# Thirteen up-projection chunks by seven products, ten of them from raw kept sums, and token sums formed in the residual's own rows

## The chip, the cores and the metric

One core of a Trainium2 chip runs the whole block. Its engines work side by side from their own queues: TensorE (PE, with weight loads PEld), VectorE (DVE), ScalarE (ACT), GpSimd (POOL) and SyncE (SP, which here only issues DMAs). The metric is the device time of one execution in microseconds, the median of several.

## The reference, cut to what matters

One layer of an encoder block over 512 frames of width 1024, all in float32. The change lies in the last line but one, and in what prepares it.

```python
def conv_glu(x, w_up, conv_w, conv_b, w_down):
    hid = x @ w_up                                  # (512 x 1024) @ (1024 x 5632)
    hid = causal_depthwise_conv3(hid, conv_w) + conv_b
    gate, up = hid[..., :2816], hid[..., 2816:]
    return (silu(gate) * up) @ w_down

def reference(x, ...):
    proj = rms_norm(x, norm1_g) @ w_in
    out_a = chunked_attention(...)                  # 8 heads
    out_b = stick_breaking_attention(...)           # 8 heads
    mixed = sigmoid(gate_a) * (out_a @ w_branch_a) + sigmoid(gate_b) * (out_b @ w_branch_b)
    x = x + mixed @ w_out
    x = x + conv_glu(rms_norm(x, norm2_g), w_ffn_up, ffn_conv_w, ffn_conv_b, w_ffn_down)
    return x
```

## The kernel before

Every float32 matrix is split into a rounded half (`hi`, by an ACT cast) and a remainder (`lo`, by a DVE subtraction), and a product is three PE products: hi by hi, hi by lo, lo by hi. Weights come in chunks of 1 MB through `load` (SP), are split by `split_gen` one chunk ahead, while the chunk before is multiplied, and are used by a body; `run_chunk` advances the split by one piece at each `yield` of the body. The order of instructions on each engine is fixed when the kernel is built, by a scheduler that goes by priority and its own estimate of times.

**Stages.** Input projection and both attentions (to about 300 us), the branch and output projections (`yB`, `wo`, to 378), the second norm with transposes (`norm_T`), the up-projection (22 chunks `up0` to `up21`, 378 to 606), the down-projection (606 to the end).

**The up-projection.** Chunk `up{j}` holds 128 columns of the gate and the same 128 of the up half. A plain chunk (`up_body`) computes both over 512 tokens: 2 x 8 blocks x 3 products of 512 columns. A chunk in `SEVEN` (`up_seven`) treats the pair as a 2 x 2 block matrix (halves of the contraction by gate and up) and the tokens as two halves of 256, and computes it with seven block products instead of eight: 7 x 4 x 3 products of 256 columns. It needs sums of weight blocks and sums of token blocks.

**Sums of weights, "parking".** In the attention stage `park_gen` loads each chunk of `SEVEN`, forms four sums on DVE and stores them in the DRAM tensor `parked`. Most chunks pass through one buffer, `pkr`; later odd ones through `pks`. `park()` takes one step at a time, at low priority, 44 times in attention, then twice at each yield of `yB` and `wo`. For a chunk in `SUMS` three of the sums are stored raw (6 steps); for the others they are stored already split (8 steps). In the up stage `fetch_extra` brings them back into a pair of buffers (`w2h`, `w2l` for chunks in `SECOND`, else `wxh`, `wxl`), one chunk ahead of the split if the buffers' last user is at least three chunks back, otherwise at the split's start; `split_seven` then splits raw ones, with two more casts and two more subtractions.

**Sums of tokens.** `norm_T` transposes the normalised rows, `xn`, into `ps`, splits them into `hth` and `htl`, and copies `ps` once more, into `xf`, which POOL stores in the DRAM tensor `htd`. `token_sums` loads it again as `xT` (SP), forms four sums (DVE) and splits them into the four `ts` tiles. `late["ts"]` is this generator, advanced at points of `up0` to `up3`. The residual rows `x2` are stored in DRAM (`x2d`, SP) and read again near the end; their place (`xs` in the pool `cp`) is given up when the pools of the attention stage close, and the pool `fp` is laid over them.

**After a chunk.** `conv` takes three taps (one on ACT, two on DVE); the gate goes to `cg`, of which there is one, and through SiLU; `up_fin` multiplies into `ub`. For each pair of chunks `pair_sums` prepares the down-projection's inputs `ax`, `ay`: `sums` on DVE at once (they use the one tile `st`), and the split, `by_dma`, as a debt in `owed` that `pay()` settles later: eight ACT copies and four POOL DMAs that add in place. In a seven-product chunk ACT saves three partial products in `pc`; `behind` keeps other ACT work that is named there (weight casts, a debt's copies) after these copies.

Of the kernel before, what the change touches and what calls it, by code (L numbers as in the profile page):

```python
# [8 lines left out]
F32 = mybir.dt.float32  # L9
# [58 lines left out]

SEVEN = (4, 5, 7, 8, 10, 11, 13, 14, 16, 17, 18, 20)
SUMS = (11, 13, 14, 16, 17, 18, 20)  # L70
SECOND = (5, 8, 11, 14, 17)


@with_exitstack
def block_kernel(ctx: ExitStack, tc: tile.TileContext, x, xt, params, g2, rbx, wts, wd0, wd1, out):
# [9 lines left out]
    hp = h_ctx.enter_context(tc.tile_pool(name="hp", bufs=1, side="right"))  # L85
    cp = ap_ctx.enter_context(tc.tile_pool(name="cp", bufs=1))

# [230 lines left out]
    dram = ctx.enter_context(tc.tile_pool(name="dram", bufs=1, space=bass.MemoryType.DRAM))  # L318
    htd = dram.tile([NT, 2, P, S], F32, tag="htd", name="htd")
    ayd = dram.tile([7, P, 1536], F32, tag="ayd", name="ayd")  # L320
# [41 lines left out]
    def norm_T(src, xn, gain, t, psum, nm):  # L362

        ss = pool_c.tile([P, 1], F32, tag="ss", name=f"ss_{nm}{t}", bufs=2)
        dump = pool_st.tile([P, D], F32, tag="skh", name=f"dump_{nm}{t}", bufs=2)
        A.activation(dump, src, AF.Square, accum_out=ss)
        rs = rstd_of(ss, 1, D, f"rs_{nm}{t}")
        for b in range(2):
            cs = slice(b * 512, (b + 1) * 512)
            V.scalar_tensor_tensor(xn[:, cs], src[:, cs], rs[:, 0:1], gain[b], op0=ALU.mult, op1=ALU.mult)  # L370
            ps = psum(f"tp_{nm}{t}{b}")
            for k in range(4):
                PE.transpose(ps[:, k * P:(k + 1) * P], xn[:, (4 * b + k) * P:(4 * b + k + 1) * P], ident)
            p3 = ps.rearrange("p (k q) -> p k q", k=4)
            hv = hth[:, 4 * b:4 * b + 4, t * P:(t + 1) * P]
            A.copy(hv, p3)
            V.tensor_tensor(htl[:, 4 * b:4 * b + 4, t * P:(t + 1) * P], p3, hv.bitcast(F32), op=ALU.subtract)

            xf = pool_wk.tile([P, S], F32, tag="wa", name=f"xf_{nm}{t}{b}", bufs=5)
            A.copy(xf, ps)  # L380
            G.dma_start(htd[t, b], xf)

# [634 lines left out]
    def pair_sums(i):  # L1017
# [5 lines left out]
        if i < 8:  # L1023
            ax = fp.tile([P, 2048], F32R, tag="ax", name=f"ax{i}", bufs=6)
            ay = fp.tile([P, 1536], F32R, tag="ay", name=f"ay{i}", bufs=2)
# [47 lines left out]
    def keep_place(i):  # L1073
# [6 lines left out]
        if ("t", j) not in keep:  # L1080
            keep["t", j] = fp.tile([P, 2048], F32, tag=("w2l", "ax")[j], name=f"t2_{j}", bufs=(1, 6)[j])
        return keep["t", j][:, (i - 3) % 4 * 512:(i - 3) % 4 * 512 + 512]

    def up_fin(j, pg, pu, g=None):
# [5 lines left out]
        if j % 2 == 1 and j // 2 < 9:  # L1090
# [8 lines left out]
            owed.append(rest_)  # L1099
            if j == 17:  # L1100
                owed.pop()()

# [8 lines left out]
    def up_body(j):  # L1111
        def body(hi, lo):
            pg, pu = BANK(f"pg{j}", j - 1), BANK(f"pu{j}", j - 1)
            yield from up_mm(pg, hi, lo, 0, 0, S)
            g = gate(j, pg)
            if j in (2, 3):
                next(late["ts"])
            held = [] if j + 1 in SEVEN else None
# [8 lines left out]
            else:  # L1127
                end()
            if j % 2 == 0:
                pay()  # L1130
            if j in (2, 3):
                next(late["ts"])
        return body

    def fetch(i):

        tag = {0: "wxh", 1: "wxl", 6: "ax"}.get(i, "ts")
        n, bufs = {"wxh": (1600, 1), "wxl": (1600, 1), "ts": (2048, 4), "ax": (2048, 6)}[tag]
        ay = fp.tile([P, n], F32R, tag=tag, name=f"ay{i}", bufs=bufs)[:, 0:1536]
# [7 lines left out]
    def token_sums():  # L1147

        x = []
        for i in range(2):  # L1150
            x.append(fp.tile([P, 2, 1024], F32, tag="ax", name=f"xT{i}", bufs=6))
            for t in range(2):
                for b in range(2):
                    SP.dma_start(x[i][:, b].rearrange("p (k q) -> p k q", k=4)[:, :, t * P:(t + 1) * P],
                                 htd[2 * i + t, b].rearrange("p (k q) -> p k q", k=4))
        b11, b21, b12, b22 = x[0][:, 0], x[0][:, 1], x[1][:, 0], x[1][:, 1]
        yield
        V.tensor_tensor(b22, b22, b12, op=ALU.subtract)
# [7 lines left out]
        for i, src in ((1, b12), (3, b22), (2, b11), (4, b21)):  # L1166
            t = fp.tile([P, 2, 1024], F32R, tag="ts", name=f"ts{i}", bufs=4)
            A.copy(t[:, 0], src)
            V.tensor_tensor(t[:, 1], src, t[:, 0].bitcast(F32), op=ALU.subtract)
            ts[i] = [t[:, j].rearrange("p (k q) -> p k q", k=4) for j in range(2)]  # L1170
            yield

    def up_seven(j):
        def body(hi, lo, wh, wl):
# [31 lines left out]
            yield  # L1206
            if j % 2 == (j - j % 2 in SEVEN and j - j % 2 + 1 in SEVEN):
                late["copied"] = (third,)
                pay()
# [20 lines left out]
    def up_first(j):  # L1230
        def body(hi, lo):
# [4 lines left out]
            if j == 1:  # L1236
                n = 0
                for i, (h, l, g, u) in enumerate(halves):
                    for o, ps in ((0, g), (P, u)):
                        for _ in up_mm(ps, h, l, o, 256, S):  # L1240
                            n += 1
                            if n == 1 or 4 <= n < 8:
                                next(late["ts"])
                            yield
# [57 lines left out]
    def fin0(p):  # L1302
# [3 lines left out]
        if p != 5:  # L1306
            tmp["k"] = fp.tile([P, 4, S], F32, tag="ax", name=f"k{p}", bufs=6)
        tmp[p] = tmp["k"][:, 2:4, :] if p == 5 else tmp["k"][:, 0:2, :]
# [72 lines left out]
    def steps1():  # L1381
        tmp["x"] = [fp.tile([P, 2, D], F32, tag="ax", name=f"x_{r}", bufs=6) for r in range(2)]
        for t in range(NT):
# [74 lines left out]
```

## Time and profile before

| | us |
|---|---|
| median of three runs (714.78 to 715.87) | 715.56 |
| the profiled execution | 717.0 |
| its span, first to last instruction | 715.3 |
| PE busy / DVE / ACT / POOL in the span | 708.5 / 588.7 / 431.7 / 85.9 |
| up-projection, from the first product of `up0` to the first of the down-projection | 378.0 to 605.8 |

The granted clock of TensorE was 0.999 of full speed. Busy times are unions of intervals; PE's are modelled and overlap, so that 99% doesn't say that no gap is left: gaps are read from what the weight loads waited for, and from the starts of consecutive products. A row of instructions reads: line, engine, operation, output <- inputs by tile name, sizes, count, then the busy time in us and the mean in ns, then the idle time of the engine ahead of them and who ended it. A row of a timeline reads: start, length, engine, line, operation, tiles, count, and the idle time ahead of it in brackets. A row by stretch gives, for each of PE, PEld, DVE, ACT and POOL, the busy time and the count, then the clock, the DMA engines' share and GB/s. In the list of waits the numbers are the total in us, how many, and the longest.

### The profile page before, as it was taken

The numbers are of one execution on the slowest core, as the hardware profiler recorded it, in microseconds if no ns is written. First come the engines' busy times: TensorE is split into PE (matmuls) and PEld (weight loads), VectorE is DVE, ScalarE is ACT, GpSimd is POOL, SyncE is SP. The second block draws the span as 40 slices with busy tenths as digits, with TensorE's granted clock in tenths as the row PEclk, the third lists the DMA queues.
The fourth block names the chain that finished last, engine by engine and source line by source line (L and its number), as shares of the span: only waits on it lengthen the run. The fifth ranks groups of instructions, "written<-read, shape, count | busy, mean of one in ns | idle before, by whom it ended". The sixth has DMA issues, their size and how long they took to land.

```text
span 715.3 us, 11278 instructions
## 1 busy us (share of the span) xinstructions
PE 708.5 (99%) x4091; PEld 622.1 (87%) x4091; DVE 588.7 (82%) x1049; ACT 431.7 (60%) x803; POOL 85.9 (12%) x123
## 2 busy tenths in 40 slices
PE   9999999999999999999999999999999999999997
PEld 7889998888988888888889989899899988888885
DVE  6668878796999999769566599698898878998686
ACT  6576656667876776434236457777877765544531
POOL 2501200000121211000003001220311111000000
PEclk9999999999999999999999999999999999999999
DMA  8722235444434383685957857998987799564563
GB/s 318 267 97 89 80 127 187 181 163 159 177 122 161 131 296 119 220 308 185 359 223 294 278 194 271 328 328 263 284 260 195 214 277 398 200 235 173 178 208 118
DMA packets 51864, 154.98 MB, mean 217 GB/s; under 512 B 5600, under 2 KB 12384, under 8 KB 44000
## 3 DMA queue, kind: packets, MB, share of 16 engines
q1 hardware_dynamic: 44256, 133.67, 52.7%
q0 software_dynamic: 7264, 20.45, 10.8%
q8 instruction: 32, 0.52, 0.3%
q14 instruction: 24, 0.20, 0.1%
q10 hardware_dynamic: 288, 0.14, 0.1%
HBM read 116.49 MB, written 30.41 MB: 205 GB/s over the span
## 4 chain that ended last, share of the span: by engine, by line
PE 87%; DVE 5%; DMA 2%; ACT 2%; issue 1%; SPq 1%; POOL 0%; DVEq 0%; ACTq 0%
PE P L1291 15%; PE p L1185 12%; PE vA L440 3%; PE uA L440 3%; PE gB L307 2%; PE qkB L309 2%; PE gB L308 2%; PE gB L309 2%; PE qkB L307 2%; PE qkB L308 2%; PE wo L308 2%; PE wo L309 2%; PE wo L307 2%; PE gA L307 2%; PE gA L308 2%; PE gA L309 2%
## 5 line engine op out<-in xcount | busy, mean ns | idle before, releaser
L172 ACT CAST whi_dn<-raw_dn 128x1024 fp32r<-128x1024 f32 x33 | 34.3, 1051 | 24.8 <-PE P L1291 20.4
L168 DVE TENSOR_TENSOR wlo_dn<-raw_dn,whi_dn 128x1024 fp32r<-128x1024 f32 x33 | 40.0, 1223 | 5.8 <-ACT whi_dn L172 5.8
L1291 PE MATMUL P<-whi_dn,ax 128*128 128x512 f32 x144 | 44.5, 389 | 0.0
L1291 PE MATMUL P<-whi_dn,ay 128*128 128x512 f32 x132 | 40.8, 389 | 0.0
L744 POOL TENSOR_SCALAR_AFFINE_SELECT bB<-bB 128x128 f32<-128x128 f32 x32 | 21.8, 686 | 143.6 <-DVE bB L743 135.0
L214 DVE TENSOR_TENSOR pkr<-pkr 128x512 f32<-128x512 f32 x40 | 27.5, 687 | 9.0 <-issue 4.7
L1185 PE MATMUL p<-ts,whi_up 128*128 128x256 f32 x192 | 34.1, 277 | 0.2 <-ACT pc L1203 0.2
L308 PE MATMUL pg<-htl,whi_up 128*128 128x512 f32 (+1 forms) x96 | 34.0, 354 | 0.0
L309 PE MATMUL pg<-hth,wlo_up 128*128 128x512 f32 (+1 forms) x96 | 33.9, 353 | 0.0
L307 PE MATMUL pg<-hth,whi_up 128*128 128x512 f32 (+1 forms) x96 | 33.8, 353 | 0.0
L1291 PEld LDWEIGHTS P<-whi_dn,ax 128*128 128x128 f32 x144 | 27.0, 188 | 5.6
L308 PE MATMUL pu<-htl,whi_up 128*128 128x512 f32 (+1 forms) x90 | 31.5, 350 | 0.0
L307 PE MATMUL pu<-hth,whi_up 128*128 128x512 f32 (+1 forms) x90 | 31.5, 350 | 0.0
L309 PE MATMUL pu<-hth,wlo_up 128*128 128x512 f32 (+1 forms) x90 | 31.4, 349 | 0.0
L1185 PEld LDWEIGHTS p<-ts,whi_up 128*128 128x128 f32 x192 | 29.2, 188 | 0.7 <-ACT pc L1203 0.4
L1291 PEld LDWEIGHTS P<-whi_dn,ay 128*128 128x128 f32 x132 | 24.8, 188 | 5.1
L250 DVE TENSOR_TENSOR wlo_up<-raw_up,whi_up 128x1024 fp32r<-128x1024 f32 x24 | 29.0, 1221 | 0.3 <-ACT whi_up L249 0.3
L742 DVE TENSOR_TENSOR_SCAN aB<-aB,reset 128x127 f32<-128x127 f32 (+3 forms) x32 | 25.9, 818 | 2.6 <-ACT aB L737 2.5
L1291 PE MATMUL P<-wlo_dn,ax 128*128 128x512 f32 x72 | 28.0, 389 | 0.0
L1185 PE MATMUL p<-hth,whi_up 128*128 128x256 f32 x96 | 26.8, 279 | 0.7 <-ACT pc L1195 0.7
L283 DVE TENSOR_TENSOR wlo_up<-raw_up,whi_up 128x1024 fp32r<-128x1024 f32 (+1 forms) x26 | 24.6, 974 | 2.8 <-ACT whi_up L278 2.7
L1185 PE MATMUL p<-hth,wlo_up 128*128 128x256 f32 x96 | 26.5, 276 | 0.0
(350 smaller groups left out, 2542.3 us busy)
## 6 DMA issues: line engine op xcount, KB each, us to landing
parked<-pkr SPq DMA_DIRECT2D x45, 256.0 KB, 2.5
raw_dn<-in_wd SPq DMA_DIRECT2D x11, 1024.0 KB, 4.8
pkr<-in_wts SPq DMA_DIRECT2D x10, 1024.0 KB, 6.9
raw_up<-in_wts SPq DMA_DIRECT2D x10, 1024.0 KB, 7.5
raw_up<-in_wts SPq DMA_DIRECT2D x12, 512.0 KB, 6.2
raw_dn<-in_wd SPq DMA_DIRECT2D x11, 512.0 KB, 3.6
wxl_up<-parked SPq DMA_DIRECT2D x21, 256.0 KB, 6.0
ayd<-ay POOLq DMA_DIRECT2D x7, 768.0 KB, 5.9
```

Of the source, the lines that this page charges most:

```text
L168: chain("halves", V.tensor_tensor(o, x, y, op=op))
L172: chain("casts", A.copy(hi[:, sl], src))
L214: V.tensor_tensor(b[o], b[x], b[y], op=op)
L250: V.tensor_tensor(l[:, sl], src[:, sl], h[:, sl].bitcast(F32), op=ALU.subtract)
L283: V.tensor_tensor(lo[:, sl], raw[:, sl], hi[:, sl].bitcast(F32), op=ALU.subtract)
L307: ins = PE.matmul(ps, sh, mh, start=first, stop=False)
L308: PE.matmul(ps, sh, ml, start=False, stop=False)
L309: PE.matmul(ps, sl, mh, start=False, stop=last)
L440: PE.matmul(pss[t], st[:, 4 * half + k, t * P:(t + 1) * P], mv[:, k, :], start=half == 0 and k == 0 and j == 0, stop=half == 1 and k == 3 ...
L742: V.tensor_tensor_scan(ar, ar, reset[:, S - n:S - 1][:, ::-1], 1.0, op0=ALU.mult, op1=ALU.max)
L1185: mm = PE.matmul(ps, st, mv[:, k, :], start=first and k == 0 and n == 0, stop=last and k == 3 and n == 2, skip_group_check=True)
L1291: chain("products", PE.matmul(dst, st, mv, start=first and n == 0, stop=last and n == 2, skip_group_check=True))
```

## The change

Chunk 12 joins `SEVEN`. Chunks 8, 10 and 12 join `SUMS`: their sums are kept raw. `SECOND`, which chunk uses which pair of buffers, is dealt anew. `htd`, its stores and its loads go: `norm_T` copies the transposed block into the residual's own rows (`src`, which is `x2`), and `token_sums` takes its blocks from there, with all its steps in the second half of `up1`. The pool `cp` stays open; its place `xs` later holds `ax4` and `ax5` together and then the residual that is read again, and the ring `ax` has four places instead of six. The conditions under which `pay()` is called are new.

```diff
-SEVEN = (4, 5, 7, 8, 10, 11, 13, 14, 16, 17, 18, 20)
-SUMS = (11, 13, 14, 16, 17, 18, 20)
-SECOND = (5, 8, 11, 14, 17)
+SEVEN = (4, 5, 7, 8, 10, 11, 12, 13, 14, 16, 17, 18, 20)
+SUMS = (8, 10, 11, 12, 13, 14, 16, 17, 18, 20)
+SECOND = (5, 8, 11, 13, 16, 18)
...
-    cp = ap_ctx.enter_context(tc.tile_pool(name="cp", bufs=1))
+    cp = ctx.enter_context(tc.tile_pool(name="cp", bufs=1))
...
-    htd = dram.tile([NT, 2, P, S], F32, tag="htd", name="htd")
...
-            xf = pool_wk.tile([P, S], F32, tag="wa", name=f"xf_{nm}{t}{b}", bufs=5)
-            A.copy(xf, ps)
-            G.dma_start(htd[t, b], xf)
+            A.copy(src[:, cs], ps)
...
-            ax = fp.tile([P, 2048], F32R, tag="ax", name=f"ax{i}", bufs=6)
+            if i == 4:
+                keep["ax"] = cp.tile([P, 4096], F32R, tag="xs", name="ax45")
+            if i in (4, 5):
+                ax = keep["ax"][:, 2048 * (i - 4):2048 * (i - 3)]
+            else:
+                ax = fp.tile([P, 2048], F32R, tag="ax", name=f"ax{i}", bufs=4)
...
             owed.append(rest_)
-            if j == 17:
-                owed.pop()()
...
-            if j in (2, 3):
-                next(late["ts"])
...
-            if j % 2 == 0:
+            if j % 2 == 0 and j + 1 not in SEVEN or j == 19:
                 pay()
-            if j in (2, 3):
-                next(late["ts"])
...
     def token_sums():
-        x = []
-        for i in range(2):
-            x.append(fp.tile([P, 2, 1024], F32, tag="ax", name=f"xT{i}", bufs=6))
-            for t in range(2):
-                for b in range(2):
-                    SP.dma_start(x[i][:, b].rearrange("p (k q) -> p k q", k=4)[:, :, t * P:(t + 1) * P],
-                                 htd[2 * i + t, b].rearrange("p (k q) -> p k q", k=4))
-        b11, b21, b12, b22 = x[0][:, 0], x[0][:, 1], x[1][:, 0], x[1][:, 1]
-        yield
+        b11, b21, b12, b22 = [x2[:, 2 * i:2 * i + 2, 512 * b:512 * b + 512] for i in range(2) for b in range(2)]
...
         for i, src in ((1, b12), (3, b22), (2, b11), (4, b21)):
             t = fp.tile([P, 2, 1024], F32R, tag="ts", name=f"ts{i}", bufs=4)
-            A.copy(t[:, 0], src)
-            V.tensor_tensor(t[:, 1], src, t[:, 0].bitcast(F32), op=ALU.subtract)
+            hi, lo = (t[:, j].rearrange("p (k t q) -> p t k q", k=4, t=2) for j in range(2))
+            src = src.rearrange("p t (k q) -> p t k q", k=4)
+            A.copy(hi, src)
+            V.tensor_tensor(lo, src, hi.bitcast(F32), op=ALU.subtract)
...
-            if j % 2 == (j - j % 2 in SEVEN and j - j % 2 + 1 in SEVEN):
+            if (j % 2 or j + 1 not in SEVEN) and j < 18:
                 late["copied"] = (third,)
                 pay()
...
-                            if n == 1 or 4 <= n < 8:
-                                next(late["ts"])
+                            next(late["ts"])
                             yield
...
-        tmp["x"] = [fp.tile([P, 2, D], F32, tag="ax", name=f"x_{r}", bufs=6) for r in range(2)]
+        x = cp.tile([P, 2, 2, D], F32, tag="xs", name="x_")
+        tmp["x"] = [x[:, r] for r in range(2)]
```

The other tiles of the ring `ax` (`t2_1`, `ay6`, the `k` tiles) get four places in the same way. By the new conditions debts are paid in chunks 2, 5, 7, 8, 11, 13, 14, 17 and 19; before, in 2, 5, 6, 8, 11, 12, 14, 17 and at the end of 17.

More of the change, by code (lines that the diff above doesn't have):

```diff
@@ L1080, in keep_place @@
         if ("t", j) not in keep:
-            keep["t", j] = fp.tile([P, 2048], F32, tag=("w2l", "ax")[j], name=f"t2_{j}", bufs=(1, 6)[j])
+            keep["t", j] = fp.tile([P, 2048], F32, tag=("w2l", "ax")[j], name=f"t2_{j}", bufs=(1, 4)[j])
         return keep["t", j][:, (i - 3) % 4 * 512:(i - 3) % 4 * 512 + 512]
@@ L1137, in fetch @@
         tag = {0: "wxh", 1: "wxl", 6: "ax"}.get(i, "ts")
-        n, bufs = {"wxh": (1600, 1), "wxl": (1600, 1), "ts": (2048, 4), "ax": (2048, 6)}[tag]
+        n, bufs = {"wxh": (1600, 1), "wxl": (1600, 1), "ts": (2048, 4), "ax": (2048, 4)}[tag]
         ay = fp.tile([P, n], F32R, tag=tag, name=f"ay{i}", bufs=bufs)[:, 0:1536]
@@ L1306, in fin0 @@
         if p != 5:
-            tmp["k"] = fp.tile([P, 4, S], F32, tag="ax", name=f"k{p}", bufs=6)
+            tmp["k"] = fp.tile([P, 4, S], F32, tag="ax", name=f"k{p}", bufs=4)
         tmp[p] = tmp["k"][:, 2:4, :] if p == 5 else tmp["k"][:, 0:2, :]
```

## The prediction

> **What bounds the kernel now.** I read the page's head, then the chain by engine, then tables by stretch, then the waits of TensorE.
>
> ```profile
> span 715.3 us, 11278 instructions
> PE 708.5 (99%) x4091; PEld 622.1 (87%) x4091; DVE 588.7 (82%) x1049; ACT 431.7 (60%) x803; POOL 85.9 (12%) x123
> PE 87%; DVE 5%; DMA 2%; ACT 2%; issue 1%; SPq 1%; POOL 0%; DVEq 0%; ACTq 0%
> 550.00:570.00 20.00, 20.00 (x178) 20.00 (x178) 17.99 (x30) 16.04 (x30) 3.45 (x4) 1.00 0.65 205
> 610.00:650.00 40.00, 40.00 (x178) 33.13 (x177) 38.33 (x51) 18.49 (x22) 1.06 (x2) 1.00 0.60 202
> 547.79 0.28 PE L1185 MATMUL p<-ts,wxl_up 128*128 128x256 f32 x1
> 548.81 0.28 PE L1185 MATMUL p<-ts,wlo_up 128*128 128x256 f32 x1
> ```
>
> TensorE (PE) is busy throughout and the chain runs through it for 87%, so time is won in two ways only: fewer products, or fewer gaps between them. Products follow each other at a pace; their printed 0.28 us overlaps. From 547.79 to 548.81 nine 256-column products start: 0.1133 us each. The two stretches hold the same 178 products, of 256 columns in 20 us and of 512 columns in 40 us, at clock 1.00, so a 512-column product takes 0.2267.
>
> Where does PE wait in the up-projection? These are the waits of the weight loads from 423 to 606 us; the lines are the copies `pc` by which ScalarE (ACT) saves a partial product.
>
> ```profile
> PEld p L1185 <- ACT pc L1195: 1.1, 2, 0.7
> PEld p L1185 <- ACT pc L1203: 0.4, 1, 0.4
> PEld p L1185 <- ACT pc L1199: 0.3, 1, 0.3
> ```
>
> That is 1.8 us: 1.1 in chunk 4 (0.4, 0.3, 0.4) and 0.7 in chunk 7. I call chunk j what the program calls `up{j}`.
>
> **Part 1: chunk 12 by seven products.** A plain chunk is 2 x 8 x 3 = 48 products of 512 columns: 10.88 us. A seven-product chunk is 7 x 4 x 3 = 84 of 256: 9.52 us. The difference, 1.36 us, comes off the bound engine: -1.36, and no row gives a way to lose it on PE itself. The Trainium skill speaks against it: TensorE: Matmul & The Clock Gate, section Back-to-back issue gap, gives a sustained spacing of 81 ns at 128 columns and 131 ns at 512, so halving the columns doesn't halve the time. Between them my estimate for 256 is 98 ns: 84 x 98 = 8.2 against 48 x 131 = 6.3 us, a loss of 1.9 us. The two stretches above show exact halving here, so I give that rule no chance.
>
> **Part 2: raw kept sums for 8, 10 and 12.** In the attention stage (parking) 8 and 10 lose three casts and three subtractions each, 12 gains four sums. VectorE (DVE) has 4 - 6 = -2 instructions there, ACT -6, SP's queue six 256 KB stores fewer but a 1024 KB load and four stores more. Attention's PE waits for none of it: 0, but for the end of parking (part 5). In exchange chunks 7, 9 and 11 get the casts and subtractions of the next chunk's sums, and 12 its five sums.
>
> ```profile
> L250 DVE TENSOR_TENSOR w2l_up<-w2l_up,w2h_up 128x1024 fp32r<-128x1024 f32 x3 | 3.6, 1216 | 0.0
> L250 DVE TENSOR_TENSOR w2l_up<-w2l_up,w2h_up 128x512 fp32r<-128x512 f32 x3 | 2.1, 686 | 0.0
> L1211 DVE TENSOR_TENSOR hu<-p,pc 128x256 f32<-128x256 f32 x12 | 5.0, 420 | 0.1
> L992 DVE SCALAR_TENSOR_TENSOR cg<-hg,par,cg 128x511 f32<-128x511 f32 x12 | 9.0, 748 | 2.5 <-ACT cg L990 2.4
> L249 ACT CAST wxh_up<-wxl_up 128x512 fp32r<-128x512 f32 x4 | 2.5, 620 | 0.0
> L249 ACT CAST wxh_up<-wxl_up 128x1024 fp32r<-128x1024 f32 x4 | 4.2, 1053 | 0.0
> L1203 ACT COPY pc<-p 128x256 f32<-128x256 f32 x12 | 4.5, 374 | 0.0
> 454.60:605.80 151.20, 150.66 (x1083) 140.86 (x1082) 129.84 (x204) 108.41 (x186) 30.09 (x39) 1.00 0.92 285
> 545.40:574.70 29.30, 29.30 (x257) 29.17 (x256) 26.03 (x42) 21.91 (x40) 4.01 (x5) 1.00 0.69 204
> ```
>
> DVE: 3 x (1.22 + 0.69) + 5 x 0.42 = 7.8 us; ACT: 3 x (1.05 + 0.62) + 4 x 0.37 = 6.5. From 454.6 to 605.8 DVE goes from 129.8 of 151.2 (86%) to 137.6 of 149.3 (92%), ACT from 72 to 77%. The cover is DVE's idle time, and it is uneven: 10 to 14 become five such chunks in a row, where before there were at most three (16 to 18). In chunks 10 to 13 DVE has three casts' remainders of 1.22 and one of 0.69, five sums, four taps of 0.75, a product of 0.69 and half a pair's four sums: 11.0 us by durations, some 9.7 by pace (sixteen instructions that overlap by 0.08, as the four of 0.68 do that take 2.48 in part 5), against 9.52 of PE. Four such chunks lose 0.7 us. If DVE also idles as in 16 to 18 (29.30 - 26.03 = 3.3 in three chunks, 1.1 each) it ends 5.1 us behind, less about 2 that it has spare in the plain chunk 9. Bounds: 0 to 3.1. I take +0.4, near the lower end: in the last stretch quoted PE is busy 29.30 of 29.30, under the same load, and a bank of PSUM is wanted again only two chunks later.
>
> Late fetches: 12, 13, 14 and 18 take buffers used two chunks earlier, so their sums are loaded only in the chunk before; now 18 and 20 do.
>
> ```profile
> 554.22 0.80 SPq L237 DMA_DIRECT2D wxl_up<-parked  x2
> 559.22 1.06 ACT L249 CAST wxh_up<-wxl_up 128x1024 fp32r<-128x1024 f32 x1
> ```
>
> For 18 the load is issued at 554.2 and cast at 559.2 without a wait; the chunk starts near 564.5. Slack 5 us less a cast and a subtraction: 0.
>
> **Part 3: token sums in place.** The eight stores to `htd` (POOL) and eight loads `xT` (SP) go; the eight ACT copies stay, with another target; the sums' twelve instructions keep their sizes, in runs of 128 elements or more.
>
> ```profile
> 394.24 6.43 SPq L1154 DMA_DIRECT2D xT<-htd  x8
> 406.54 1.23 DVE L1158 TENSOR_TENSOR xT<-xT 128x1024 f32<-128x1024 f32 x1 [4.87 <-DMA xT<-htd]
> 390.40:406.50 16.10, 16.10 (x124) 15.29 (x123) 5.52 (x9) 7.42 (x11) 1.09 (x2) 1.00 0.78 232
> 427.83 0.77 ACT L990 ACTIVATE ub<-pu,par 128x512 f32<-128x512 f32 x1
> 428.51 0.62 ACT L1014 ACTIVATE cg<-cg 128x512 f32<-128x512 f32 x1
> 429.03 0.36 ACT L1195 COPY pc<-p 128x256 f32<-128x256 f32 x1
> 386.93 1.27 ACT L380 COPY xf_n<-tp_n 128x512 f32<-128x512 f32 x2
> 377.90 1.76 SPq L941 DMA_DIRECT2D x2d<-x  x2
> DMA to landing us min/median/max: 2.7/4.6/5.9
> ```
>
> Before, the first sum starts at 406.54, held 4.87 us by the reload that SP issues from 394.24 on. Now the rows are ready when the last copy ends, near 391. In 390.4 to 406.5 DVE is busy 5.52 of 16.10, so 10.6 us stand free, and the sums' eight DVE instructions of 1.23 need 9.8. DVE's queue after 406.5, which held up the taps and SiLU that stand ahead of the first `pc` copy on ACT (429.03, behind the SiLU of 428.51), shrinks by about that. So chunk 4's 1.1 us should go: -1.1, bounds 0 (ACT is blocked by something else) and -1.1. What is late next is chunk 7.
>
> The change adds a wait: the copy into the residual's rows must wait until the store of these rows (`x2d`, the last line: its landings) has read them. The last two are issued from 377.90 on and the second by 379.7; at most 5.9 later, 385.6, they have landed; the copies come at 386.93. Slack 1.3 us, and behind the copy on ACT stands the next cast of the transposed input, for which PE waits. Bounds 0 to 2 (a landing as late as that again by half), taken as 0. With the stores, POOL loses eight issues and SP eight; what SP issues next (the first kept sums, read from chunk 4 on) comes earlier, and nobody waits for it: 0. The residual's 16 KB are kept and later hold `ax4`, `ax5` and the reloaded residual, while the ring `ax` has four places for six; `ax6` and `ax7` follow `ax0` and `ax1`, which go to DRAM as before: 0.
>
> **Part 4: the order of the debts (`pay`).** Pair 2's split (eight ACT copies, four accumulating DMAs) moves from chunk 6 into chunk 7, behind the third `pc`.
>
> ```profile
> 447.19 9.50 DMA ay<-st
> 456.82 0.44 DVE st L1044
> 461.19 0.52 ACT cg L1014
> 461.70 0.27 ACT pc L1195
> ```
>
> This is the chain up to the 0.7 us gap: an accumulating DMA of 9.50 us frees `st`, DVE forms the pair's sums, ACT's copies of the debt follow, then a SiLU, then `pc` at 461.70, and PE. The debt leaves that queue; the wait for `st` and the SiLU behind DVE stay. Bounds 0 and -0.7; I take -0.5, since eight ACT copies stood between `st` and `pc` and one SiLU remains. The other debts move between seven-product chunks of like load; chunks 11 and 13 will carry a debt and a full split, which chunk 17 carries now inside the stretch without gaps: 0. Pair 8's debt moves from the end of 17 to 19, where ACT ran it anyway.
>
> **Part 5: the end of parking.** All parked chunks but the last odd ones pass one buffer, `pkr`, and DVE serves it in its order.
>
> ```profile
> 338.37 0.33 SPq L209 DMA_DIRECT2D pkr<-in_wts  x1
> 355.35 0.33 SPq L209 DMA_DIRECT2D pkr<-in_wts  x1
> 362.55 1.42 DVE L214 TENSOR_TENSOR pkr<-pkr 128x512 f32<-128x512 f32 x2 [4.71 <-issue]
> 363.89 0.68 DVE L939 TENSOR_TENSOR x<-wo,x 128x512 f32<-128x512 f32 x1
> 374.79 2.48 DVE L377 TENSOR_TENSOR htl<-tp_n,hth 128x512 fp32r<-128x512 f32 x4
> 378.12 0.28 PE L308 MATMUL pg<-htl,whi_up 128*128 128x256 f32 x1
> ```
>
> DVE stands idle 4.71 us until 362.55 for the last parked load, and behind it in its queue wait the additions to the residual (363.89), the norm, the transposes and `htl`, which ends at 377.27; PE reads it at 378.12. Slack 0.85 us, so an earlier end gains nothing, and a later one costs its lateness less 0.85. By the program's steps there were 5 x 8 + 7 x 6 = 82, now 3 x 8 + 10 x 6 = 84, and the last pass through `pkr` begins at step 78 instead of 70; but the shorter entries 8 and 10 bring the buffer further ahead: four passes remain after step 42, as they did after step 40. Two steps of a pass of 17.0 us (338.37 to 355.35) in six are 5.7 us late at worst: bounds 0 to 4.8, taken as 0, since the buffer's own pace, the same four passes, sets the end.
>
> **Sum.** -1.36 - 1.1 - 0.5 + 0.4 = -2.56 us. The profiled execution took 717.0 us (span 715.3), so it would take 714.4; the median, 715.56, lies 1.4 below it, and I forecast 713.0. A measurement can tell about 0.2%, 1.4 us: faster is below 714.1, slower above 717.0.
>
> **Rivals.** (a) The reasons for the gaps stay (the sums are placed on DVE as late as before; ACT is blocked elsewhere), and only the products go: 715.56 - 1.36 = 714.2, on the edge. For it: DVE's order is fixed ahead, and the sums are issued in chunk 1's second half in the program; against it: 10.6 free us. (b) DVE's five full chunks: half of the 5.1 us reaches PE, 2.6 less the 0.4 in the sum: 715.2, no change. For it, 9.7 us of work against 9.52; against it, three such chunks without a gap. (c) Slower: the last parked load comes late. From 0.85 + 2.56 = 3.4 us of lateness on it eats the whole gain; from 4.8 on it is slower by over 0.2%, and at 5.7 the time is 713.0 + 4.8 = 717.8. For it: one pass more, and DVE already waits there; against it: 8 and 10 are shorter.
>
> **Chances.** Forecast 0.54, (a) 0.15, (b) 0.17, (c) 0.14. Faster takes the forecast and half of (a): 0.61; same takes the other half of (a), 0.15 of (b) and 0.04 of (c): 0.27; slower, 0.12, is the rest of (c) and (b)'s upper end. Range: low 711.9, all gains and no new loss (712.4) less half a us for the runs' spread; high 716.4, which holds (b) and leaves out most of (c). The forecast's own range is 711.9 to 714.1.
>
> **What would show it.** Right: 84 products in chunk 12; the first token sum near 391 to 395; no weight load waiting for `pc` in chunk 4 and under 0.3 us in chunk 7; DVE at about 92% from chunk 7 on. Wrong: gaps before `pc`-bound products in 10 to 14 (b), PE idle near 378 with DVE waiting for `pkr` (c), the first sum after 400 (a), ACT idle before the copies into the residual's rows.

## The result, and the profile after

The changed kernel takes 725.80 us (median of 4 runs, 724.0 to 727.98) against 715.71 (714.78 to 716.12): ratio 1.0145, interval 1.0130 to 1.0161. It is 10 us slower where 713.0 was forecast and 716.4 was the range's end. The profiled execution took 724.0 us, the fastest of the four; before it was 717.0, 1.3 above its median. So the two traces differ by 7.0 us where the medians differ by 10.1, and some 3 us of the loss lie in runs that no trace shows. The head of the page:

```profile
span 722.3 us, 11310 instructions
PE 709.3 (98%) x4127; PEld 622.8 (86%) x4127; DVE 594.0 (82%) x1058; ACT 435.5 (60%) x807; POOL 81.8 (11%) x115
```

PE has 36 products more (84 for 48), as it should. What its weight loads waited for, from 424 to 630 us and from 230 to 260 us (total, how often, longest):

```profile
PEld P L1280 <- ACT whi_dn L172: 2.5, 1, 2.5
PEld p L1175 <- ACT pc L1193: 2.1, 1, 2.1
PEld p L1175 <- ACT pc L1185: 0.9, 1, 0.9
PEld p L1175 <- DVE wlo_up L250: 0.9, 2, 0.7
PEld p L1175 <- DVE wxl_up L250: 0.7, 1, 0.7
PEld p L1175 <- ACT w2h_up L249: 0.4, 1, 0.4
PEld p L1175 <- ACT wxh_up L249: 0.3, 1, 0.3
...
PEld pT_B L757 <- POOL bB L741: 1.6, 1, 1.6
```

The four old waits in chunks 4 and 7 are gone; nine new ones stand elsewhere. To place them I take every product's distance to the next, less its pace (0.1133 us for 256 columns, 0.2267 for 512), and sum what is over by stretch:

| us of the span | before | after | |
|---|---|---|---|
| 0 to 25 | 3.06 | 2.20 | start; one and the same other kernel showed 2.28 and 3.15 |
| 225 to 250 | 1.65 | 3.13 | branch B's attention |
| 425 to 475 | 2.29 | 0.09 | chunks 4 and 7 |
| 500 to 575 | 0.18 | 3.86 | chunks 11 to 17 |
| 575 to 600 | 0.08 | 2.29 | chunk 20 |
| 600 to 625 | 0.00 | 4.00 | first down product |
| all | 25.66 | 34.32 | |

+8.66 less the 1.36 of fewer products is +7.3; the spans differ by 7.0. So the gains came, and four new losses of 1.5 to 4 us each came with them.

**Chunks 11 to 13.** ACT's timeline from the end of chunk 12 on (PE begins chunk 13 near 513.4), SP's queue before it, and the time from issue to landing of its three `w2l` DMAs:

```profile
513.97 1.05 ACT L249 CAST w2h_up<-w2l_up 128x1024 fp32r<-128x1024 f32 x1 [2.83 <-DMA w2l_up<-parked]
517.52 0.62 ACT L249 CAST w2h_up<-w2l_up 128x512 fp32r<-128x512 f32 x1 [2.50 <-DMA w2l_up<-parked]
518.04 0.37 ACT L1205 COPY hg<-p 128x256 f32<-128x256 f32 x1
...
519.64 0.37 ACT L1185 COPY pc<-p 128x256 f32<-128x256 f32 x1
```
```profile
503.60 0.33 SPq L148 DMA_DIRECT2D raw_up<-in_wts  x1
503.97 0.43 SPq L149 DMA_DIRECT2D raw_up<-parked  x1
504.45 0.45 SPq L150 DMA_DIRECT2D raw_up<-in_wts  x1
505.00 2.18 SPq L237 DMA_DIRECT2D w2l_up<-parked  x3
```
```profile
DMA to landing us min/median/max: 7.7/8.0/10.8
```

ACT stands 5.3 us for chunk 13's kept sums, which should have been split before chunk 13 began, and in its order `hg`, the debt's copies and the `pc` of 519.64 stand behind them; PE waits for that `pc`. The sums were issued behind the three loads of the next raw weights, and landed 7.7 to 10.8 us after their issue (last row, of these three DMAs).

**Chunk 20 and the end.** DVE and, at the end, ACT, with PE by stretch (busy time and count of PE, PEld, DVE, ACT, POOL; clock; DMA share; GB/s):

```profile
591.34 1.42 DVE L168 TENSOR_TENSOR raw_dn<-raw_dn 128x512 f32<-128x512 f32 x2 [4.87 <-DMA raw_dn<-in_wd]
...
607.94 0.69 DVE L168 TENSOR_TENSOR raw_dn<-raw_dn 128x512 f32<-128x512 f32 x1 [1.38 <-DMA raw_dn<-in_wd]
608.55 0.68 DVE L1091 TENSOR_TENSOR ub<-cg,ub 128x512 f32<-128x512 f32 x1
...
613.89 0.75 DVE L990 SCALAR_TENSOR_TENSOR ub<-pu,par,ub 128x510 f32<-128x510 f32 x1
```
```profile
594.83 0.63 ACT L1011 ACTIVATE cg<-cg 128x512 f32<-128x512 f32 x1 [5.06 <-DVE cg L990]
...
596.30 0.36 ACT L1193 COPY pc<-p 128x256 f32<-128x256 f32 x1
...
609.33 0.78 ACT L987 ACTIVATE cg<-pg,par 128x512 f32<-128x512 f32 x1 [5.10 <-PE pu L309]
```
```profile
612.00:615.00 3.00, 0.89 (x4) 0.45 (x4) 1.83 (x3) 3.00 (x5) 0.00 (x0) 1.00 0.49 205
615.00:619.50 4.50, 4.50 (x14) 3.51 (x14) 4.47 (x7) 1.71 (x3) 0.00 (x0) 0.62 0.12 15
```

Twice DVE stands in order for a load of down-projection weights that nobody needs yet, while the taps, SiLU and product behind it set when `pc` is copied and when a bank of PSUM comes free. At 591.34 (4.87 us) it makes chunk 20's third `pc` late: PE loses 2.1 us at 594.5. At 607.94 it holds chunk 20's product (608.55), which frees the one `cg`, which chunk 21's gate needs (609.33); its last tap ends at 614.64 and frees the bank that PE has wanted since 612.5. The page names `whi_dn` there, whose cast had ended at 614.00; the bank came last. Behind this gap the granted clock is 0.62 over 4.5 us: 3.4 us at half speed, products 0.43 us apart, another 1.7 us lost (4.00 in that stretch less the gap's 2.28).

### The profile page after: what moved, and what is told of

It is laid out like the page before. It is cut to its first block, busy times and chain, and to the rows that moved or that the text cites. A ratio compares the mean times of both kernels' runs of the same rounds, so it can differ in the third digit from the quotient of the medians.

```text
span 722.3 us, 11310 instructions
## 1 busy us (share of the span) xinstructions
PE 709.3 (98%) x4127; PEld 622.8 (86%) x4127; DVE 594.0 (82%) x1058; ACT 435.5 (60%) x807; POOL 81.8 (11%) x115
## 4 chain that ended last, share of the span: by engine, by line
PE 76%; DVE 9%; DMA 7%; ACT 3%; issue 2%; SPq 1%; POOL 1%; DVEq 0%; ACTq 0%; POOLq 0%
PE P L1280 14%; PE p L1175 8%; PE vA L437 3%; DMA w2l_up<-parked 3%; PE uA L437 3%; DMA raw_dn<-in_wd 3%; PE gB L309 2%; PE gB L307 2%; PE gB L308 2%; PE wo L307 2%; PE wo L308 2%; PE wo L309 2%; PE gA L307 2%; PE gA L309 2%; PE gA L308 2%
## 5 line engine op out<-in xcount | busy, mean ns | idle before, releaser
L214 DVE TENSOR_TENSOR pkr<-pkr 128x512 f32<-128x512 f32 x44 | 30.2, 686 | 12.4 <-DMA pkr<-in_wts 12.2
L1175 PE MATMUL p<-ts,whi_up 128*128 128x256 f32 x208 | 37.4, 277 | 1.9 <-ACT pc L1193 1.9
L309 PE MATMUL pg<-hth,wlo_up 128*128 128x512 f32 (+1 forms) x88 | 30.8, 350 | 0.0
L307 PE MATMUL pg<-hth,whi_up 128*128 128x512 f32 (+1 forms) x88 | 30.8, 350 | 0.0
L308 PE MATMUL pg<-htl,whi_up 128*128 128x512 f32 (+1 forms) x88 | 30.7, 349 | 0.0
L249 ACT CAST whi_up<-raw_up 128x1024 fp32r<-128x1024 f32 x26 | 27.0, 1054 | 3.2 <-PE pu L308 2.8
L308 PE MATMUL pu<-htl,whi_up 128*128 128x512 f32 (+1 forms) x83 | 28.8, 347 | 0.0
L307 PE MATMUL pu<-hth,whi_up 128*128 128x512 f32 (+1 forms) x83 | 28.8, 347 | 0.0
L1175 PE MATMUL p<-htl,whi_up 128*128 128x256 f32 x104 | 28.7, 276 | 0.0
L309 PE MATMUL pu<-hth,wlo_up 128*128 128x512 f32 (+1 forms) x83 | 28.7, 346 | 0.0
```

Of the source, the lines that this page charges most:

```text
L214: V.tensor_tensor(b[o], b[x], b[y], op=op)
L249: behind(A.copy(h[:, sl], src[:, sl]), late["pcs"])
L307: ins = PE.matmul(ps, sh, mh, start=first, stop=False)
L308: PE.matmul(ps, sh, ml, start=False, stop=False)
L309: PE.matmul(ps, sl, mh, start=False, stop=last)
L1175: mm = PE.matmul(ps, st, mv[:, k, :], start=first and k == 0 and n == 0, stop=last and k == 3 and n == 2, skip_group_check=True)
```

## Experiments

Five theories were to be told apart. L: kept sums fetched only one chunk ahead land late. D: DVE is overloaded by five seven-product chunks in a row. T: the end is lost to DVE waiting in order for a load. And the parts of the change that were priced at 0: raw sums in the attention stage (R), debts (B). Each kernel was timed against the kernel before on its own chip, which took 715.0 to 715.8 there, so a difference between variants of different chips is uncertain by some tenths of a us. Times are medians; what a trace shows is of one execution.

**One part alone: token sums in place** (the edit is the whole of the `htd`, `xf`, `token_sums`, `late["ts"]`, `cp` and `ax` hunks above, on the kernel before).

> The kernel before with part 3 alone (token sums in place, the ring and the pool that go with it); SEVEN, SUMS, SECOND and the debts as before. By the prediction's step the 1.1 us of gaps in chunk 4 go and the 0.7 us in chunk 7 stays: 715.7 - 1.1 = 714.6, the first token sum near 391 to 395. If keeping the rows costs something elsewhere (an ACT copy waiting for the store of the rows, the memory plan), it is 715.7 or more.

713.78 us, ratio 0.9982 (0.9972 to 0.9991); once more on another chip 714.05, ratio 0.9974 (0.9964 to 0.9984). No weight load from 230 to 640 us waits for anything. The gap of chunk 7 went too, though the debts were left as before: that gap was the DVE queue's as chunk 4's was, not the debt's. This version has the lowest median of all and beats both kernels; the best two with chunk 12 come within its interval.

**The whole change without chunk 12.**

```diff
-SEVEN = (4, 5, 7, 8, 10, 11, 12, 13, 14, 16, 17, 18, 20)
-SUMS = (8, 10, 11, 12, 13, 14, 16, 17, 18, 20)
-SECOND = (5, 8, 11, 13, 16, 18)
+SEVEN = (4, 5, 7, 8, 10, 11, 13, 14, 16, 17, 18, 20)
+SUMS = (8, 10, 11, 13, 14, 16, 17, 18, 20)
+SECOND = (5, 8, 11, 14, 17)
```

> The changed kernel with chunk 12 plain again and the buffers dealt as before (SECOND of before, so only 18 and 20 are fetched late); raw sums for 8 and 10, token sums in place and the new debts stay. Theory L (the sums of 12, 13, 14 land late, and ACT stands in its queue for them) and theory D (five chunks with full splits overload DVE) both say: no gaps from chunk 10 on, gaps of 4 and 7 gone, 715.7 - 1.8 = 713.9 or a little less. If the raw sums or the new debts are the cause, it stays above 718.

720.71, ratio 1.0074 (1.0055 to 1.0093): 7 us worse than the token sums alone. With no new late fetch it still has the gap near 248 (1.3 us), waits for `pc` in 520 to 564 (2.3) and 2.2 at the end. L and D both expected 713.9. So raw sums or debts, which I had priced at 0, cost; two tests further down part them.

**Without the late fetches** (a constant stands in place of the sums of 12, 13, 14 and 18, so that these chunks' results are not the reference's).

```diff
+        if j in (12, 13, 14, 18):
+            G.memset(wl.bitcast(F32), 0.01)
+            extras[j] = wh, wl
+            return
```

> The changed kernel; the sums of 12, 13, 14 and 18 are not fetched from DRAM, POOL fills their buffers with a constant instead (so these four chunks compute with wrong sums), and every cast, subtraction and product stays. Theory L: the 3.5 us of gaps in 10 to 14 go, and with them, if the lag is handed on, the gaps of 2.1 us in chunk 20 and 2.3 us at the first down product: 712 to 714; if it is not handed on, 720 to 722. Theory D: the gaps stay, 724 to 727.

716.04 (714.27 to 721.15), ratio 1.0020 (0.9999 to 1.0040). ACT and DVE do all their casts and subtractions, and the gaps in chunks 11 to 13 and at chunk 20 are gone; left are 1.7 us at 248 and 2.7 at the first down product. The time lies between the two ranges that L allowed. For the gaps that went D falls and L stands: it is when the sums land, not the work on them.

**The reload of `ax0` one chunk later**, since in the run of the change it shared the DMA engines with the late `raw_dn`.

```diff
-        if j in (SECOND[-1] + 1, SEVEN[-1] + 1):
+        if j in (SECOND[-1] + 2, SEVEN[-1] + 1):
```

> The changed kernel with the reload of ax0 (1 MB) issued after chunk 20 instead of after chunk 19. Theory E (this reload, which the new SECOND moved beside the load of the first down weights, makes these land late, 9.0 us instead of 7.8): the wait of DVE for the first down weights falls from 4.9 us to 3 or less, the gap in chunk 20 to under 1 us, 722 to 724. Theory L with the lag handed on: the load is issued late already, little changes there, 725 to 727.

724.79, ratio 1.0133 (1.0115 to 1.0151), within the spread of the whole change; the gap at chunk 20 stays (2.6 us). So that transfer's place is not the cause.

**Raw sums alone, debts alone** (each on the token sums in place).

```diff
-SUMS = (11, 13, 14, 16, 17, 18, 20)
+SUMS = (8, 10, 11, 13, 14, 16, 17, 18, 20)
```
```diff
-            if j == 17:
-                owed.pop()()
...
-            if j % 2 == 0:
+            if j % 2 == 0 and j + 1 not in SEVEN or j == 19:
...
-            if j % 2 == (j - j % 2 in SEVEN and j - j % 2 + 1 in SEVEN):
+            if (j % 2 or j + 1 not in SEVEN) and j < 18:
```

> The kernel before with the token sums in place (713.8 us, no gap from chunk 4 on) plus one thing: chunks 8 and 10 join SUMS, so their sums are kept raw and split again in chunks 7 and 9. The variant with these raw sums and the new debts together took 720.7. Theory R (the raw sums carry that loss): the gap of 1.3 to 1.7 us near 248 comes back, because the order on DVE in the attention stage is another, and the up-projection shows gaps of 1 us or more in all at the copies pc; 717 or more. Theory B (the new debts carry it): no gap near 248 and none at the pc copies, within 1 us of 713.8.

> The kernel before with the token sums in place (713.8 us) plus one thing: the new conditions under which debts are paid, pair 8's in chunk 19 instead of the end of 17 among them. Theory B: the accumulating DMAs of the moved debts stand beside the loads of raw weights and ACT meets them ahead of pc copies; gaps in chunks 11 to 14 (0.5 to 1 us), and a gap of 1 to 2 us at the first down product; 716 to 719. Theory R: within 1 us of 713.8, and no gap over 0.4 us after chunk 4. Either way nothing changes near 248.

Raw sums: 715.80, ratio 1.0015 (1.0005 to 1.0025), 2.0 above the token sums alone. Debts: 715.67, ratio 1.0005 (0.9994 to 1.0016), 1.9 above them. Both are less than R (717 or more) and B (716 to 719) expected. The waits of PE's weight loads from 230 to 640 us, first of the raw sums, then of the debts:

```profile
PEld pT_B L757 <- POOL bB L741: 1.4, 1, 1.4
```
```profile
PEld p L1175 <- ACT pc L1185: 1.3, 1, 1.3
```

R is right about 248 us, wrong about the `pc` copies. B's part is one gap, in chunk 16 at 548 and not in 11 to 14, and behind it a slower pace: until 571.6 products of 256 columns start 0.118 us apart, at a granted clock of 1.00, which loses 0.8 us more. The row by stretch has 172 products where the kernel before had 178:

```profile
550.00:570.00 20.00, 20.00 (x172) 20.00 (x171) 18.64 (x31) 17.02 (x31) 3.19 (x4) 1.00 0.69 224
```

Why 248: DVE's order, first after the change, then before.

```profile
246.08 0.67 DVE L214 TENSOR_TENSOR pkr<-pkr 128x512 f32<-128x512 f32 x1
246.68 1.27 DVE L283 TENSOR_TENSOR wlo_gB<-raw_gB,whi_gB 128x512 fp32r<-128x512 f32 x2
247.89 0.67 DVE L740 TENSOR_TENSOR bB<-bB,aB 128x511 f32<-128x511 f32 x1
```
```profile
244.77 0.68 DVE L743 TENSOR_TENSOR bB<-bB,aB 128x511 f32<-128x511 f32 x1
245.37 1.28 DVE L283 TENSOR_TENSOR wlo_gB<-raw_gB,whi_gB 128x512 fp32r<-128x512 f32 x2
246.58 0.68 DVE L214 TENSOR_TENSOR pkr<-pkr 128x512 f32<-128x512 f32 x1
```

With fewer steps for 8 and 10, other parking sums fall due here and stand ahead of the product `bB` (POOL masks it, PE transposes it), which comes 3.1 us later. The two parts add up to 3.9 of the 7 us that they cost together; the 2.2 at the end came only with both, and why is not shown.

**Chunk 12 alone, and then with its fetch first in SP's queue** (both on the token sums in place, old debts, 8 and 10 split; by this `SECOND` six chunks, 12, 13, 14, 16, 18 and 20, are fetched late, where the change has four).

```diff
-SEVEN = (4, 5, 7, 8, 10, 11, 13, 14, 16, 17, 18, 20)
-SUMS = (11, 13, 14, 16, 17, 18, 20)
-SECOND = (5, 8, 11, 14, 17)
+SEVEN = (4, 5, 7, 8, 10, 11, 12, 13, 14, 16, 17, 18, 20)
+SUMS = (11, 12, 13, 14, 16, 17, 18, 20)
+SECOND = (5, 8, 11, 13, 17)
```
```diff
...
         if is_seven(i) and i - pos["up0"] not in extras:
             fetch_extra(i - pos["up0"])
+            while postponed:
+                next(load(postponed.pop()))
...
-        if nxt is not None and nxt < len(order):
-            next(load(nxt))
+        if nxt is not None and nxt < len(order):
+            if j in SEVEN and not early:
+                postponed.append(nxt)
+            else:
+                next(load(nxt))
```

> The kernel before with the token sums in place (713.8 us) plus chunk 12 by seven products with raw sums, buffers dealt so that 12, 13 and 14 take theirs two chunks after the last user; the debts stay as before and 8 and 10 are kept split. Theory L (kept sums fetched only one chunk ahead land after their casts' turn): ACT idles 2 us or more for a parked piece in chunks 11 to 13, PE loses 2 to 3 us there, and the 1.36 us of fewer products are lost again: 714 to 716. Rival N (no loss here, the five chunks in a row are harmless with the old debts): 712.4.

> As the variant with chunk 12 alone by seven products, with one change: where kept sums are fetched only one chunk ahead, SyncE issues them before the next chunk's raw weights and not behind them (in the run of the whole change chunk 13's fetch stood 3.2 us behind three raw loads that waited for their buffer). Theory Q (the place in SyncE's queue makes them late): landings come about 3 us earlier, the idle time of ACT at the parked pieces falls under 1 us in each chunk, and the time falls 1 to 3 us below the variant without this, to 712.4 to 713.5. Theory S (the transfers themselves, 8 to 10 us from issue to landing, make them late): the idle time stays, within 0.7 us of the variant without this; the raw weights, issued later, may then be the next to be late.

Chunk 12 alone: 722.16, ratio 1.0098 (1.0072 to 1.0124). With the fetch first: 719.80 (715.44 to 721.93), ratio 1.0053 (1.0027 to 1.0078). Both are some 6 us above what L and Q expected (714 to 716, and 712.4 to 713.5): in the profiled runs PE lost 4.9 us from 500 to 575 and 1.8 at the end without the order, 0.1 and 5.5 with it, and neither theory had the end. Chunk 13's fetch, first without the order: SP's issues and ACT's first cast in the timeline, then the time from issue to landing of the three DMAs.

```profile
501.64 0.32 SPq L237 DMA_DIRECT2D w2l_up<-parked  x1
502.38 0.33 SPq L148 DMA_DIRECT2D raw_up<-in_wts  x1
...
504.14 0.95 SPq L237 DMA_DIRECT2D w2l_up<-parked  x2
...
513.26 1.05 ACT L249 CAST w2h_up<-w2l_up 128x1024 fp32r<-128x1024 f32 x1 [5.19 <-DMA w2l_up<-parked]
```
```profile
DMA to landing us min/median/max: 4.4/9.0/12.1
```

With it first:

```profile
502.23 1.86 SPq L237 DMA_DIRECT2D w2l_up<-parked  x3
...
507.59 1.06 ACT L249 CAST w2h_up<-w2l_up 128x1024 fp32r<-128x1024 f32 x1 [0.35 <-DMA w2l_up<-parked]
```
```profile
DMA to landing us min/median/max: 4.3/4.6/5.8
```

Of the landings Q is right, S wrong: two of three pieces stood behind 1 MB of raw weights, waited in SP's queue and then shared the DMA engines with it. First in the queue, the three land in 4.3 to 5.8 us, and no weight load from 424 to 600 us waits for anything. The profiled run now loses only at the end, 3.8 us and 1.7 of half clock behind it.

**The end: two subtractions moved.**

```diff
         if n < NP:
+            if n == 1:
+                late["halves"] += late["gtap"]     # chunk 21's last gate tap
             sub(b[:, 3], b[:, 3], b[:, 2])
             sub(b[:, 2], b[:, 2], b[:, 0])
...
+        late["gtap"] = late["tap2"]                # tap2: the second tap on DVE
```

> The variant with token sums in place, chunk 12 by seven and the late fetches issued first (profiled run 719.8), with two DVE instructions moved: the two subtractions on the second down-projection chunk (raw_dn, 2 x 0.69 us) stand behind chunk 21's gate taps and no longer ahead of chunk 20's product. Nothing else on any queue changes but two casts of ACT that follow. Theory T (the end is lost because DVE waits in order for that load, 2.03 us at 601.92, ahead of the work that frees chunk 21's bank): the gap of 3.76 us at 606 falls under 1.5 us, the stretch of half clock behind it goes, and the time falls to 714.3 or, with the start of the kernel as short as in the better runs, to 712.5. Rival U (DVE is late at the end anyhow, from the load of chunks 12 to 20): the gap stays over 2 us and the time within 1.5 us of 719.8.

> The whole change, with only the two subtractions on the second down-projection chunk moved behind chunk 21's gate taps. Theory T: the gap of 2.28 us at 612.28 and the 1.6 us of half clock behind it go, and the gaps near 248, in chunks 11 to 13 and of 2.08 us at 594.5 stay: 725.8 - 4 = 721.8. Rival U: 725 to 726, with the gap at the end in its place.

> The whole change with both mends: the late fetches issued ahead of the next raw weights, and the two subtractions moved. If the theories of the late fetch and of the end are all there is beside the gap near 248, PE's lost time after 500 falls from 10 us to under 1, the 1.6 us near 248 stay, and the time is 713.8 (before) - 1.36 + 1.6 = 714 to 715.5. If the new debts cost by themselves, as the variant with them alone showed (1.3 us at 548), 716 to 718 with a gap at a pc copy in chunks 14 to 17 or at 594.

The two subtractions now stand behind chunk 21's gate taps. On chunk 12 with its fetch first: 714.50, ratio 0.9991 (0.9979 to 1.0002), 5.3 less; the gap is 0.5 and the clock full. On the whole change: 721.74, ratio 1.0083 (1.0063 to 1.0103), 4.1 less; the gap at the end is gone, those at 248, 521 to 528 and 594 stay. With the fetch order too: 715.26, ratio 1.0000 (0.9991 to 1.0010), 6.5 less again. Its waits from 230 to 640 us:

```profile
PEld pT_B L767 <- POOL bB L751: 1.3, 1, 1.3
PEld p L1186 <- ACT pc L1200: 0.4, 1, 0.4
PEld p L1186 <- ACT pc L1196: 0.3, 1, 0.3
```

T and Q together account for 10.5 of the 12 us between the whole change and the token sums alone. Chunk 20's gap went with the order: `raw_dn` lands at 584.74 there, not at 591.32.

**What is left of chunk 12's 1.36 us.** One more sum (`t` of the first down chunk) moved behind chunk 21's product; then also chunk 20's parked sums formed in `pks`, not `pkr`.

```diff
+            if n == 1:
+                late.pop("t0")()
             part(1024, raw[:, 1024:2048])
-            sub(t2, b[:, 3], b[:, 0], op=ALU.add)
+            if n == 0:
+                late["t0"] = lambda: sub(t2, b[:, 3], b[:, 0], op=ALU.add)
+            else:
+                sub(t2, b[:, 3], b[:, 0], op=ALU.add)
...
-            if late.get("heads") and m % 2:
+            if late.get("heads") and (m % 2 or m == 12):
```

> The variant with token sums in place, chunk 12 by seven, late fetches first and the two subtractions moved (714.5), with one DVE instruction more moved: the sum t (0.68 us) on the first down-projection chunk, which nothing in the up-projection waits for, stands behind chunk 21's product and no longer ahead of chunk 20's. If chunk 21's bank is on the edge (in that variant PE still waited 0.35 us at 605.7, and the kernel before had 0.1 us to spare there), the 0.5 us at 605.7 go and the time is 714.0, and with the start as short as in the variant with token sums alone, 712.4 to 713; the third and fourth down chunks are then loaded some 8 us later, and if that is too late a gap of about 1 us shows near 614 or 619. If the end is not on the edge, no change: 714.5.

> The last variant (token sums in place, chunk 12 by seven, late fetches first, the end's three DVE instructions moved; 714.75), with chunk 20's parked sums formed in the buffers of the later odd chunks (pks) and no longer in pkr, so that chunk 12 adds no pass through pkr at the end of parking. Theory P (chunk 12's 1.36 us are paid back at the end of parking: there DVE waited 1.64 us for the last pkr load at 375.19 and formed its sums among the htl, and PE lost 1.4 us more near 377 than with the token sums alone): the lost time there falls to that variant's and the time to 713 (712.4 to 713.5). Rival V (the 1.36 us go elsewhere, or the sums of 20, now among the branch projection, are late instead): 714 to 715, with a gap elsewhere, near 330 to 378 or in chunk 20's fetch.

> The kernel before with the token sums in place and nothing else, once more, on the chip of the variant beside it, for a direct comparison: 713.8 again. Theory P: 0.5 to 1.4 us slower than the variant with chunk 12 and pks; rival V: as fast or faster.

The sum moved: 714.75, ratio 0.9991 (0.9980 to 1.0002), no gain. The loss at the end is nearly gone (0.15 us), but in this run PE lost 1.4 us more from 370 to 410 than with the token sums alone. Of this 0.9 stand near 377, where DVE forms the sums of an added last pass through `pkr`, and the rest behind it, up to 395:

```profile
375.19 0.69 DVE L221 TENSOR_TENSOR pkr<-pkr 128x512 f32<-128x512 f32 x1 [1.64 <-DMA pkr<-in_wts]
```

With `pks`: 720.11, ratio 1.0058 (1.0045 to 1.0072), slower. DVE stands in its order 3.8 us for `pks` and, until 322.0, 2.2 for `pkr`, ahead of the additions of `yB` to `gb` (from 323.81) that free PE's bank: PE lost 3.7 us at 320.7 and was then at half clock; from 370 to 410 it lost 0.8 less. The gap elsewhere is rival V's, the time is 5 us above what V expected.

Where the 1.36 us go can be read from two traces whose starts are nearly alike, the token sums the second time (span 712.6) and the two subtractions moved (712.9). Of the latter's +0.3, -1.36 are products and -0.2 the start; +0.5 are lost from 370 to 410, where products of 256 columns start 0.118 us apart until 389.7 and not only until 385.1, and where two gaps of 0.1 follow at 391; +0.6 at the first down product; and +0.75 behind the last product, from whose start it takes 5.09 us to the end of the span and not 4.33. This last part is the same in all five variants of chunk 12 with old debts (5.05 to 5.09). At the very end each of their traces has a transfer of the queue that the profile calls instruction, and the token sums' traces have none; that this is its cause is not shown.

## Why the prediction was wrong, by its own steps

- **Part 1, -1.36: right on PE**, 84 products at the pace read before. It is no net gain in any variant; the last experiment says where it goes.
- **Part 3, -1.1: right.** The first token sum starts at 392.07 (forecast 391 to 395), chunk 4's gaps went, no copy waited for `x2d`. **Chunk 7's -0.5** was right in sign and under its size (0.8 with what follows) by luck: the token sums cured it, with the debts as they were.
- **Part 2, "Slack 5 us less a cast and a subtraction: 0": failed, the first large term.** I read the first of three pieces. In the kernel before, the third stood behind a raw load and its cast came just in time:

```profile
554.22 0.80 SPq L237 DMA_DIRECT2D wxl_up<-parked  x2
555.11 0.38 SPq L155 DMA_DIRECT2D raw_up<-in_wts  x1
555.54 0.43 SPq L237 DMA_DIRECT2D wxl_up<-parked  x1
...
563.79 0.61 ACT L249 CAST wxh_up<-wxl_up 128x512 fp32r<-128x512 f32 x1
```
```profile
DMA to landing us min/median/max: 2.9/3.3/8.0
```

  The third landed at 555.54 + 8.0 = 563.5, and was cast at 563.79, for a chunk that began near 564.5. The slack was 0.3, and the change fetches 12, 13, 14 and 18 like this, three of them in a row. Measured: 3.7 us in chunks 11 to 17, 2.2 at chunk 20; the place of these DMAs in SP's queue decides (6.5 us between the whole change with and without it, the end mended; 2.4 with chunk 12 alone, the end not mended).
- **Part 2, five full chunks, +0.4: too low for the whole change; rival (b)'s size came, its cause is not seen.** Five such chunks in a row alone cost nothing: with chunk 12 alone and its fetch first, PE lost 0.2 us from 458 to 603. In the whole change with fetches and end mended, DVE is busy 130.5 of 146.0 us from chunk 7 on (89%; I forecast 92) and PE lost 2.3 there, near (b)'s 2.6: 0.8 in gaps, 0.7 of them two waits for `pc` in chunk 11, ahead of which DVE worked from 491.5 to 499.2 without a pause, and 1.5 because products then start 0.118 us apart until 537. The raw sums of 8 and 10 and the debts together cost 3.0 us from 500 to 575 also without chunk 12 (second experiment), so the five in a row are not needed for it.
- **Part 2, "Attention's PE waits for none of it: 0": failed**, 1.5 us. The number of steps was fewer, but their places moved ahead of `bB`.
- **Part 4, the other debts at 0: failed** by 1.9 us alone, the gap at 548 and the slower pace behind it. In the trace of the whole change that gap doesn't appear.
- **The end: no step at all, the largest term, 4.0 us.** In the kernel before, chunk 21's last tap ends at 609.31 (first row), 3.5 us behind the first down product. The bank that it frees is wanted by the 22nd down product, whose weight load stands at 610.35 (the second of the two in the last row):

```profile
608.56 0.75 DVE L993 SCALAR_TENSOR_TENSOR ub<-pu,par,ub 128x510 f32<-128x510 f32 x1
...
610.12 0.41 PEld L1291 LDWEIGHTS P<-whi_dn,ax0b 128*128 128x128 f32 x2
```

  That it is the 22nd shows where this load had to wait, without chunk 12 by seven (the second experiment): it follows the tap's end, 613.69, by 0.11 us.

```profile
612.94 0.75 DVE L990 SCALAR_TENSOR_TENSOR ub<-pu,par,ub 128x510 f32<-128x510 f32 x1
...
613.80 0.19 PEld L1280 LDWEIGHTS P<-whi_dn,ax0b 128*128 128x128 f32 x1 [1.24 <-ACT whi_dn L172]
```

  So there were some 0.9 us to spare, and two things used them up. DVE's chain of load, subtraction, product and tap, which I never timed because nothing waited there, ended 5.5 us behind the first down product. And the bank moved. `BANK` deals the banks in turn, and chunk 12 by seven products takes two turns more from the ring that serves chunk 21: in every run with it where PE waits for this tap, the 16th product is the one that waits (in the run of the change at 614.75, again 0.11 us behind the tap's end), six products or 1.36 us earlier. No run moves the bank alone.
- **Part 5, end of parking, 0: right for the whole change** (1.20 us lost from 375 to 400 before, 1.27 after). Rival (c) didn't occur. The slower side came by other ways than (c), to which I had given most of it.

## What to carry to other kernels

Before an upstream gain is booked, time the places downstream that are on the edge already: a hand-over that shows no wait can have under 1 us to spare. Look also at which buffer of a ring falls to whom: a chunk that takes more turns can move a later chunk to a buffer that is wanted earlier. For a load in several pieces take the last landing, and look at what stands between the pieces in the issuing queue. Place instructions that wait for a far load behind the work that frees a shared buffer: two moved subtractions were worth 4 to 5 us here, the place of the fetches in the queue 6.5 with the end mended.

## What the hardware did that I had not expected

In or after some gaps of PE the granted clock fell to a half for 3.4 us; in the run of the change PE resumed at 614.78 and had the half clock from 616.03 to 619.44. Over all runs it followed gaps in which PE lost 2.3 us (here), 2.6 (twice), 3.1, 3.7 and 3.8, and did not follow 1.7, 2.1 and 2.5. The Trainium skill (TensorE: Matmul & The Clock Gate, section What's actually happening) gives an idle window of about 3.4 us for such a fall; here 2.3 was once enough, and the measurement decides. A gap near that size costs its length and some 1.7 us more. One DMA of parked sums took from 2.9 to 12.1 us to land; for the same sums of chunk 13 it was 4.4 to 12.1 with raw weights issued between them and 4.3 to 5.8 ahead of them.

Behind some shorter waits products of 256 columns started 0.118 us apart and no longer 0.113, for 22 us with the debts alone (550.0 to 571.6) and some 35 in the whole change mended, while the granted clock stood at 1.00. It costs 4% for as long as it lasts, and no list of waits shows it. What brings or ends it is not shown.
